# Eight more expert ups ahead of the dense stage, kept in row buffers

## The chip, the cores and the metric

The kernel runs on one core of a Trainium2 chip. The metric is the device time of one execution in microseconds, as the median of several runs. Engines are named as the profile names them: PE (TensorE matmuls), PEld (its weight loads), DVE (VectorE), ACT (ScalarE), POOL (GpSimd), SP (the queue that issues most transfers).

## What is computed

One decoder layer on 512 tokens of width 1024 in float32: a token sublayer (retention and forgetting attention, merged), and a channel sublayer, in which each token picks 128 of 16384 single-neuron experts by product keys. Cut to the second:

```
q  = (xc @ w_q).reshape(n, 8, 2, 128)
sc = einsum('nhcd,hckd->nhck', q, sub_keys)
s, idx = top_k(sc, 16)                       # per head and half
cand, cid = all 16 x 16 sums and expert numbers
top_s, pos = top_k(cand, 16);  eid = cid[pos];  gate = softmax(top_s)
hid = einsum('nhkd,nd->nhk', expert_u[eid], xc)
y   = einsum('nhk,nhkd->nd', gelu(hid) * gate, expert_v[eid])
h  <- LN(alpha*h + y + sigmoid(h W_g + b_g) * (p W_ple))
```

## The kernel before

The 512 tokens are four blocks of 128. The experts of the first two blocks are **gathered**: for each token and each of its 128 choices, POOL issues an indirect DMA that fetches one row of `peer_u` (128 tokens x 1024, 0.5 MB) into a row buffer, DVE multiplies it with x and sums it (L1087), later the same with `peer_v`, added to h (L1097). That makes 512 rows of each 0.5 MB. There are `ROWS` = 6 buffers "row", and, once the dense stage has begun, `MORE` = 2 further ones "more" (4 KB per partition each).

The last two blocks (256 tokens) run through **all** experts as dense products, in 128 blocks `b` of 128 experts each:

- `up(b)`: PE multiplies the block's `peer_u` with the 256 tokens (tile `hid`, 8 matmul instructions, which the trace shows as 16 records); ACT applies Gelu and writes the tile `a`. Two blocks share one 1 MB load `ur`, of which there are two buffers.
- `gate(b)`: DVE multiplies `a` with the dense gates `gw` of this block, and ACT rounds the product to `ah`.
- `load(b)` and `remainder`: ACT rounds the block's `peer_v` (1 MB load `vr` for two blocks) to `vh`, DVE writes the rest `vl`; likewise `al` from `a` and `ah`.
- `down(b)`: PE adds `ah*vh + ah*vl + al*vh` to four PSUM accumulators `acc` (12 matmuls).

The dense gates come from the routing: `select` (DVE, with a few ACT steps) makes the tiles `rt` for 128 tokens; PE transposes them (`gt`), ACT copies them to `tabs`, DVE builds one-hot masks `oa` and `ob` (`spread`), PE multiplies these (`gp`), ACT copies the products to `stg` and sends them to memory (`gd`), from where `gw` is loaded. This happens for one token block after the other.

`lead` ups are done before the dense loop, wherever `k.fill` puts them: between the query products, between the steps of `spread`, and the last four after it. `RES` = 4 more follow, straight into the accumulators' banks. The others run inside the loop over `b`. So the loop holds 128 - 44 - 4 = 80 ups.

On PE, DVE and POOL the order of instructions is that in which the code issues them. A small model in the kernel (`Clock`) keeps an estimate of the time of PE, DVE and the DMAs while the code is issued; `k.fill` issues an up when DVE is estimated over 2 us behind PE (`k.fill.when`), and `k.clock.row` issues a gathered row when DVE and the DMAs are estimated to have room. The order on ACT and SP is set by the compiler's scheduler.

Of the kernel before, what the change touches and what calls it, by code (L numbers as in the profile page):

```python
# [9 lines left out]
F32 = mybir.dt.float32  # L10
# [7 lines left out]
S, D, P = 512, 1024, 128  # L18
# [3 lines left out]
HEADS, K, NK = 8, 16, 128  # L22
# [109 lines left out]
class Clock:  # L132
# [3 lines left out]
    base, more = 0.07, 0.06  # L136
# [144 lines left out]
def norm_steps(k, dst, src, g, b, st=None, share=True):  # L281

    nc = k.nc
    mv = k.tp.tile([P, 2], F32, tag="ln_mv", name=k.uniq("mv"))
    rs = k.tp.tile([P, 1], F32, tag="ln_rs", name=k.uniq("rs"))
    if st is None:
        st = ln_tile(k)
        for i in range(2):
            ln_stats(k, st, i, src[:, i * 512:(i + 1) * 512])
        yield  # L290
    nc.vector.bn_aggr(mv, st)
    rstd(k, rs, mv[:, 1:2], 1)
    yield
    for i in (1, 0):
        sl = slice(i * 512, (i + 1) * 512)
        x = src[i] if isinstance(src, list) else src[:, sl]
        nc.vector.scalar_tensor_tensor(dst[:, sl], x, mv[:, 0:1], g[:, sl], op0=ALU.subtract, op1=ALU.mult)
        if i and share:
            nc.scalar.activation(dst[:, sl], dst[:, sl], AF.Copy, scale=rs)
            nc.gpsimd.tensor_tensor(dst[:, sl], dst[:, sl], b[:, sl], op=ALU.add)  # L300
        else:
            nc.vector.scalar_tensor_tensor(dst[:, sl], dst[:, sl], rs, b[:, sl], op0=ALU.mult, op1=ALU.add)
        yield
# [633 lines left out]
def by_slot(k, tr, routed):  # L937

    nc = k.nc
    ps = k.px.tile([P, 3, P], F32, tag="px", name=k.uniq("gt"))  # L940
    for i, src in enumerate(routed):
        nc.tensor.transpose(ps[:, i, :], src, k.ident)
    nc.scalar.activation(tr, ps, AF.Copy)
# [39 lines left out]
ROWS, MORE = 6, 2  # L983
XTRA = 2
RES = 4


class Experts:
# [7 lines left out]
    def up(self, b, ps=None):  # L996
        k, nc, ND = self.k, self.k.nc, self.ND
        if b % 2 == 0:
            self.uraw = k.us.tile([P, 2, 8, P], F32, tag="uraw", name=k.uniq("ur"))
            nc.sync.dma_start(self.uraw, k.I["uT"][b // 2])  # L1000
        if ps is None:
            ps = self.ph.tile([P, ND], F32, tag="hid", name=k.uniq("hid"))
        for c in range(8):
            nc.tensor.matmul(ps, self.uraw[:, b % 2, c, :], k.h1[:, c, :], start=c == 0, stop=c == 7)
        a = self.ap.tile([P, ND], F32, tag="a", bufs=self.lead + RES + XTRA, name=k.uniq("a"))
        nc.scalar.activation(a, ps, AF.Gelu)
        self.act[b] = a

# [91 lines left out]
def channel(k, dense, lead, ctx):  # L1100
    nc, tc, I = k.nc, k.tc, k.I
    gd = k.dr.tile([P, NK // GI, len(dense) * P // SG, GI * SG], F32, name="gd")
    ap = ctx.enter_context(tc.tile_pool(name="ap", bufs=2))
    k.us = ctx.enter_context(tc.tile_pool(name="us", bufs=2))
    ph = ctx.enter_context(tc.tile_pool(name="ph", bufs=2, space=PSUM))
    ex = Experts(k, dense, gd, lead, ap, ph)
    k.fill.items, k.fill.rate = [(ex.up, b) for b in range(lead)], 8
    k.fill.when = lambda: len(k.fill.items) > RES and k.clock.dve > k.clock.pe + 2
    k.clock.pace, k.clock.due, k.clock.base, k.clock.more = 4.2, k.clock.pe, 0.085, 0.115
    c0 = ExitStack()  # L1110
    with ExitStack() as c1:
        k.pp = c1.enter_context(tc.tile_pool(name="pp2", bufs=4, space=PSUM))
        k.px = c1.enter_context(tc.tile_pool(name="px2", bufs=2, space=PSUM))
        rp = c0.enter_context(tc.tile_pool(name="rp", bufs=2, side="right"))
        routed = [[rp.tile([P, HEADS * K], F32, bufs=1, name=f"rt{n}_{i}") for i in range(3)] for n in range(2)]
        with ExitStack() as c2:
            kp = c2.enter_context(tc.tile_pool(name="kp", bufs=2))
            s16, i16 = product_keys(k, REST, rp, kp, k.h1)
            k.side.items, k.side.rate = [select(k, rp, s16[:, 0], i16[:, 0], *routed[0])], 2.25
            embedding_gate(k, REST, k.h1, kp)  # L1120
            k.side.drain()
        with ExitStack() as c2:
            sps = [c2.enter_context(tc.tile_pool(name=f"sp{i}", bufs=1)) for i in range(2)]
            k.obs = k.slot([P, 2, 8, P], F32, "S2", "ob")
            tabs = k.fp.tile([P, 8, P], F32, tag="xg", bufs=FIRST.nt, name="tabs")
            k.iota = tabs[:, 6, :]
            nc.sync.dma_start(k.iota, I["iota"])
            k.side.items, k.side.rate = [select(k, rp, s16[:, 1], i16[:, 1], *routed[1])], 0.65
            for n in range(len(dense)):
                k.fill()  # L1130
                tr = tabs[:, 3 * n:3 * n + 3, :]
                by_slot(k, tr, routed[n])
                if n == len(dense) - 1:
                    c0.close()
                    dv = ctx.enter_context(tc.tile_pool(name="dv", bufs=2, side="right"))
                    for b in (0, 2):
                        ex.fetch(b, dv)
                for i, _ in enumerate(spread(k, sps, tr, n * P, gd, 4 if n else 8)):
                    k.clock.hold = n == len(dense) - 1 and i >= 28
                    k.tick()  # L1140
                k.side.drain()
            while k.fill.items:
                k.fill.step()
                k.clock.before()
    k.clock.before = lambda: None
    dl = ctx.enter_context(tc.tile_pool(name="dl", bufs=1))
    dp = ctx.enter_context(tc.tile_pool(name="dp", bufs=2))
    po = ctx.enter_context(tc.tile_pool(name="po", bufs=1, space=PSUM))
    acc = [[po.tile([P, 512], F32, name=f"acc{m}_{g}") for g in range(2)] for m in range(len(dense))]
    k.tp = dp  # L1150
    k.rows = [(k.gp, "row", ROWS)] * ROWS + [(k.gp, "more", MORE)] * MORE
    k.nrow = 0
    gb = k.slot([P, 2, D], F32, "S2", "gb2")
    g2, b2 = gb[:, 0, :], gb[:, 1, :]

    def finish(t):
        yield from norm_steps(k, k.h0[:, t, :], k.h0[:, t, :], g2, b2, share=False)
        nc.sync.dma_start(I["out"][t * P:(t + 1) * P, :], k.h0[:, t, :])
    for t in FIRST.blocks:
        at = max(0, len(k.feed.items) - (2 * P + 1) * (FIRST.end - 1 - t))  # L1160
        k.feed.items.insert(min(at + 24, len(k.feed.items)), finish(t))
    pace = len(k.feed.items) / (NK - 3)
    for b in range(2):
        ex.load(b, dl, dv)
    for i in range(RES):
        ex.up(lead + i, acc[i // 2][i % 2][:, :ex.ND])
    for b in range(2):
        ex.remainder(*ex.vw[b])
    k.feed(2)
    for b in range(3):  # L1170
        ex.gate(b, dl, dp)
    nc.sync.dma_start(g2, bcast(I["ln2_g"], D))
    nc.sync.dma_start(b2, bcast(I["ln2_b"], D))
    for b in range(2):
        ex.remainder(*ex.act[b])
    done = lead + RES
    for b in range(NK):
        if b + 2 < NK:
            ex.load(b + 2, dl, dv)
        while done < NK and done < lead + RES + (NK - lead - RES) * (b + 1) / (NK - 6):  # L1180
            ex.up(done)
            done += 1
        if b + 3 < NK:
            ex.gate(b + 3, dl, dp)
        k.feed(pace / 2)
        if b + 2 < NK:
            ex.remainder(*ex.vw[b + 2])
        k.feed(pace / 2)
        if b + 2 < NK:
            ex.remainder(*ex.act[b + 2])  # L1190
        if b < NK - 2:
            ex.down(b, acc, range(len(dense)))
        if b == 0:
            for m, t in enumerate(dense):
                for g in range(2):
                    nc.vector.tensor_tensor(acc[m][g], acc[m][g], k.h0[:, t, g * 512:(g + 1) * 512], op=ALU.add)
    assert not k.feed.items
    for m, t in enumerate(dense):
        for b in (NK - 2, NK - 1):
            ex.down(b, acc, (m,))  # L1200
        st = ln_tile(k)
        for g in range(2):
            ln_stats(k, st, g, acc[m][g])
        layer_norm(k, k.h0[:, t, :], acc[m], g2, b2, st=st, share=m < len(dense) - 1)
        for g in range(2):
            sl = slice(g * 512, (g + 1) * 512)
            nc.sync.dma_start(I["out"][t * P:(t + 1) * P, sl], k.h0[:, t, sl])
# [82 lines left out]
```

## Time and profile before

| | us |
|---|---|
| median of 3 runs | 1804.19 (1802.31 to 1805.01) |
| profiled execution, its own time | 1807.46 |
| its span | 1805.3 |
| PE busy | 1661.7 (92%) |
| DVE busy | 1378.1 (76%) |
| ACT busy | 600.1 (33%) |
| POOL busy | 633.2 (35%) |
| moved by DMA | 566.45 MB, 314 GB/s over the span |

Times in the trace are counted from the start of the span. The profile puts an engine's idle time down to what ended it, so "PE acc <- DVE al" is PE waiting for the tile `al` from DVE. Buffer numbers are left out there: `row` stands for every row buffer. The granted clock of PE was 0.972 on average. From 781 us on PE runs ups; the first gates' transposes start at 931 us, the second ones at 1045 us, the last `gp` ends at 1099.5 us, and the loop over the blocks begins at about 1135 us.

### The profile page before, as it was taken

To read this page: it belongs to the slowest core of one execution; us is meant where nothing else is said; L and a number is where in the kernel's file an instruction comes from. 1 tells how busy PE (TensorE), PEld (TensorE's weight loads), DVE (VectorE), ACT (ScalarE), POOL (GpSimd) and SP (SyncE) were. 2 spreads that over 40 slices of the span, in tenths; PEclk is the share of its full clock that TensorE was granted. 3 is DMA by queue.
4 is the path that set the end of the run, shared out by engine and by line. 5 is a ranking of instruction groups with operands and counts; after the bars stand their busy time and mean duration, and the time that the engine had idled before them with its cause. 6 is when DMAs were issued, how large, how long until landed. Compare 5 with 4: busy or idle time off the path is not lost.

```text
span 1805.3 us, 22411 instructions
## 1 busy us (share of the span) xinstructions
PE 1661.7 (92%) x7872; PEld 1330.5 (74%) x7872; DVE 1378.1 (76%) x2688; ACT 600.1 (33%) x1098; POOL 633.2 (35%) x524
## 2 busy tenths in 40 slices
PE   6999999998799999799949977999999999999995
PEld 4888996454656886488738966888888788788783
DVE  5654464697778888678988984787788788888888
ACT  4556643221023430111026674332323322332322
POOL 1000000025657555243443301334445444445441
PEclk9999999999899999999979999999999999999998
DMA  8544455879999999788876977999999999999993
GB/s 273 170 138 133 149 162 186 252 259 358 346 328 395 374 349 400 273 331 344 313 274 227 334 255 281 377 390 401 355 414 395 396 409 395 406 396 410 383 378 139
DMA packets 152992, 566.45 MB, mean 314 GB/s; under 512 B 18096, under 2 KB 34992, under 8 KB 134448
## 3 DMA queue, kind: packets, MB, share of 16 engines
q1 hardware_dynamic: 62496, 278.73, 42.0%
q0 software_dynamic: 73872, 269.52, 38.9%
q10 hardware_dynamic: 16512, 16.78, 2.7%
q8 instruction: 62, 1.02, 0.2%
q14 instruction: 50, 0.41, 0.1%
HBM read 543.99 MB, written 20.97 MB: 313 GB/s over the span
## 4 chain that ended last, share of the span: by engine, by line
PE 51%; issue 24%; DVE 10%; DMA 8%; ACT 3%; POOL 3%; SPq 1%; ACTq 0%; DVEq 0%; POOLq 0%
PE hid L194 20%; PE acc L194 17%; PE pj L194 8%; DVE h L1097 4%; DMA row<-in_peer_v,geu 3%; POOL row L1081 2%; PE gp L194 2%; PE lg L194 2%; DMA wr<-in_w_peer_q 2%; DVE s L194 1%; DMA row<-in_peer_u,geu 1%; DVE row L1087 1%; DVE i L194 1%; ACT vh L194 1%; DMA pw<-w 1%
## 5 line engine op out<-in xcount | busy, mean ns | idle before, releaser
L1081 POOL DMA_INDIRECT row<-in_peer_v,geu x256 | 320.5, 1252 | 389.0 <-DVE h L1097 324.7
L194 PE MATMUL hid<-h1f,ur 128*128 128x256 f32 x1984 | 449.9, 381 | 0.0
L1081 POOL DMA_INDIRECT row<-in_peer_u,geu x256 | 301.9, 1179 | 382.6 <-DVE row L1087 244.4
L194 PEld LDWEIGHTS hid<-h1f,ur 128*128 128x128 f32 x1984 | 378.4, 192 | 56.3 <-issue 3.8
L1097 DVE SCALAR_TENSOR_TENSOR h<-row,ghid,h 128x1024 f32<-128x1024 f32 x256 | 327.6, 1280 | 27.2 <-DMA row<-in_peer_v,geu 24.4
L1087 DVE SCALAR_TENSOR_TENSOR row<-row,xg 128x1024 f32<-128x1024 f32 x256 | 308.0, 1217 | 26.0 <-DMA row<-in_peer_u,geu 23.5
L194 DVE TENSOR_TENSOR vl<-vr,vh 128x1024 fp32r<-128x1024 f32 x128 | 156.8, 1226 | 107.5 <-ACT vh L194 107.5
L194 PE MATMUL acc<-vh,al 128*128 128x512 f32 x512 | 203.3, 397 | 21.7 <-DVE al L194 21.6
L194 PE MATMUL acc<-vh,ah 128*128 128x512 f32 x512 | 215.7, 421 | 0.0
L194 PE MATMUL acc<-vl,ah 128*128 128x512 f32 x512 | 201.7, 394 | 1.4 <-DVE vl L194 1.4
L194 DVE TENSOR_TENSOR wl<-wr,wh 128x1024 fp32r<-128x1024 f32 x72 | 88.1, 1223 | 85.9 <-ACT wh L194 85.7
L194 ACT ACTIVATE a<-hid 128x256 f32<-128x256 f32 x124 | 47.4, 382 | 299.9 <-PE hid L194 283.7
L194 ACT ACTIVATE vh<-vr 128x1024 fp32r<-128x1024 f32 x128 | 129.8, 1050 | 20.7 <-PE acc L194 18.9
L194 ACT ACTIVATE ah<-a 128x256 fp32r<-128x256 f32 x128 | 53.1, 416 | 242.3 <-DVE a L194 212.9
L194 PEld LDWEIGHTS acc<-vh,al 128*128 128x128 f32 x512 | 96.6, 189 | 48.9 <-DVE al L194 29.3
L194 PE MATMUL pj<-wr,h1f 128*128 128x512 f32 x256 | 120.7, 613 | 6.6 <-DMA wr<-in_w_peer_q 3.0
L194 PE MATMUL pj<-hT,wr 128*128 128x256 f32 x512 | 117.0, 385 | 0.1
L194 PEld LDWEIGHTS acc<-vl,ah 128*128 128x128 f32 x512 | 97.0, 189 | 24.2 <-DVE vl L194 3.3
L194 PEld LDWEIGHTS acc<-vh,ah 128*128 128x128 f32 x512 | 97.1, 190 | 18.8
L300 POOL TENSOR_TENSOR h<-h,b 128x512 f32<-128x512 f32 x6 | 8.2, 1388 | 291.7 <-ACT h L194 274.4
L194 PEld LDWEIGHTS pj<-hT,wr 128*128 128x128 f32 x512 | 97.3, 193 | 14.0 <-issue 1.4
L194 ACT ACTIVATE wh<-wr 128x1024 fp32r<-128x1024 f32 x72 | 76.2, 1058 | 93.5 <-PE pj L194 76.8
(231 smaller groups left out, 2489.3 us busy)
## 6 DMA issues: line engine op xcount, KB each, us to landing
ur<-in_uT SPq DMA_DIRECT2D x64, 1024.0 KB
vr<-in_vP SPq DMA_DIRECT2D x64, 1024.0 KB
wr<-in_w_in SPq DMA_DIRECT2D x104, 512.0 KB
wr<-in_w_peer_q SPq DMA_DIRECT2D x48, 512.0 KB
gd<-stg ACTq DMA_DIRECT2D x8, 2048.0 KB
gw<-gd SPq DMA_DIRECT2D x15, 1024.0 KB
wr<-in_w_ret_o SPq DMA_DIRECT2D x16, 512.0 KB
wr<-in_w_out SPq DMA_DIRECT2D x16, 512.0 KB
```

The lines of the kernel that those rows point to most:

```text
L194: return f(*a, **kw)
L300: nc.gpsimd.tensor_tensor(dst[:, sl], dst[:, sl], b[:, sl], op=ALU.add)
L1081: k.tc.nc.gpsimd.indirect_dma_start(out=r, out_offset=None, in_=src, in_offset=bass.IndirectOffsetOnAxis(ap=self.e[:, c:c + 1], axis=0))
L1087: self.k.tc.nc.vector.scalar_tensor_tensor(r, r, 1.0, self.x, op0=ALU.mult, op1=ALU.mult, accum_out=self.hid[:, c:c + 1])
L1097: self.k.tc.nc.vector.scalar_tensor_tensor(h1, r, self.hid[:, c:c + 1], h1, op0=ALU.mult, op1=ALU.add)
```

## The change

`lead` becomes 52. The ups of blocks 0 to 7 are the last eight of the lead instead of the first, and their results go into two tiles of four blocks each (`slab`), which take the two buffers "more" until these blocks are past; the pool of `a` keeps its 50 buffers. Until block 8 the gather therefore has six row buffers, and from there on all eight. The loop's 72 ups start at block 6, since the buffers of `a` come free only from block 8's end on, but for two. After the selection of the first gates the clock model's DVE time is put 20 us later, which makes `k.fill` issue ups there.

```
+SLAB = 8
...
-        a = self.ap.tile([P, ND], F32, tag="a", bufs=self.lead + RES + XTRA, name=k.uniq("a"))
+        if b < SLAB:
+            if b % 4 == 0:
+                self.slab = k.gp.tile([P, 4, ND], F32, tag="more", bufs=MORE, name=k.uniq("slab"))
+            a = self.slab[:, b % 4, :]
+        else:
+            a = self.ap.tile([P, ND], F32, tag="a", bufs=self.lead - SLAB + RES + XTRA, name=k.uniq("a"))
...
-    k.fill.items, k.fill.rate = [(ex.up, b) for b in range(lead)], 8
+    k.fill.items, k.fill.rate = [(ex.up, b) for b in (*range(SLAB, lead), *range(SLAB))], 8
...
             k.side.drain()
+            k.clock.dve += 20
...
-    k.rows = [(k.gp, "row", ROWS)] * ROWS + [(k.gp, "more", MORE)] * MORE
...
     for b in range(NK):
+        if b == SLAB:
+            k.rows = [(k.gp, "more", MORE)] * MORE + [(k.gp, "row", ROWS)] * ROWS
+            k.nrow = 0
...
-        while done < NK and done < lead + RES + (NK - lead - RES) * (b + 1) / (NK - 6):
+        while done < NK and done < lead + RES + (NK - lead - RES) * (b - SLAB + 3) / (NK - SLAB - 4):
...
-        decoder_layer(tc, aps, 44)
+        decoder_layer(tc, aps, 44 + SLAB)
```

Where it moves instructions. PE at the first gates' transposes, before (`hid` is an up, x8 its eight matmul instructions):

```order
L194 MATMUL hid_6508<-h1f,ur_6465 128x256 x8
L194 MATMUL hid_6546<-h1f,ur_6544 128x256 x8
L194 MATMUL gt_6557<-ident,rt_0_5440 128x128
L194 MATMUL gt_6557<-ident,rt_1_5441 128x128
L194 MATMUL gt_6557<-ident,rt_2_5442 128x128
L194 MATMUL gp_6572<-oa_6562,ob 128x128 x4
L194 MATMUL hid_6582<-h1f,ur_6544 128x256 x8
```

and after:

```order
L194 MATMUL hid_6546<-h1f,ur_6544 128x256 x8
L194 MATMUL hid_6557<-h1f,ur_6544 128x256 x8
L194 MATMUL hid_6570<-h1f,ur_6568 128x256 x8
L194 MATMUL hid_6581<-h1f,ur_6568 128x256 x8
L194 MATMUL hid_6594<-h1f,ur_6592 128x256 x8
L194 MATMUL hid_6605<-h1f,ur_6592 128x256 x8
L194 MATMUL hid_6618<-h1f,ur_6616 128x256 x8
L194 MATMUL gt_6629<-ident,rt_0_5440 128x128
L194 MATMUL gt_6629<-ident,rt_1_5441 128x128
L194 MATMUL gt_6629<-ident,rt_2_5442 128x128
L194 MATMUL gp_6653<-oa_6634,ob 128x128 x4
L194 MATMUL hid_6663<-h1f,ur_6616 128x256 x8
```

Six ups have come between the last up of before and the transposes. DVE at the same place, from the end of `rt` to the first masks, before:

```order
L194 TENSOR_TENSOR rt_2_5442<-rt_2_5442,gsm_6530 128x128
L1097 SCALAR_TENSOR_TENSOR h_68<-row_6563,ghid_2841,h_68 128x1024
L194 TENSOR_TENSOR oa_6562<-tabs 128x1024
L194 TENSOR_TENSOR ob<-tabs 128x1024
L194 TENSOR_TENSOR oa_6568<-tabs 128x1024
```

and after (L1103 is the former L1097, a gathered row):

```order
L194 TENSOR_TENSOR rt_2_5442<-rt_2_5442,gsm_6530 128x128
L1103 SCALAR_TENSOR_TENSOR h_68<-row_6635,ghid_2841,h_68 128x1024
L1103 SCALAR_TENSOR_TENSOR h_68<-row_6638,ghid_2841,h_68 128x1024
L1103 SCALAR_TENSOR_TENSOR h_68<-row_6641,ghid_2841,h_68 128x1024
L1103 SCALAR_TENSOR_TENSOR h_68<-row_6644,ghid_2841,h_68 128x1024
L194 TENSOR_TENSOR oa_6634<-tabs 128x1024
L194 TENSOR_TENSOR ob<-tabs 128x1024
```

Three more rows stand ahead of the masks; over both spreadings six more rows are issued before the dense loop. ACT there, before (`sg` is the embedding gate's Sigmoid, the last `rt` row an Exp, `a` a Gelu):

```order
L194 ACTIVATE a_6555<-hid_6546 128x256
L194 ACTIVATE w_6460<-iff_6154 128x1024
L194 ACT_TABLE_LOAD
L194 ACTIVATE sg_6343<-sg_6343 128x512 x2
L194 ACT_TABLE_LOAD
L194 ACTIVATE rt_2_5442<-rt_2_5442 128x128
```

and after:

```order
L194 ACTIVATE a_6566<-hid_6557 128x256
L194 ACTIVATE w_6460<-iff_6154 128x1024
L194 ACTIVATE a_6579<-hid_6570 128x256
L194 ACTIVATE a_6590<-hid_6581 128x256
L194 ACTIVATE a_6603<-hid_6594 128x256
L194 ACTIVATE a_6614<-hid_6605 128x256
L194 ACT_TABLE_LOAD
L194 ACTIVATE sg_6343<-sg_6343 128x512 x2
L194 ACT_TABLE_LOAD
L194 ACTIVATE a_6627<-hid_6618 128x256
L194 ACT_TABLE_LOAD
L194 ACTIVATE rt_2_5442<-rt_2_5442 128x128
```

The last of the new Gelus stands between the Sigmoid and the Exp, with one table load more. Further on PE has 19 ups, not 18, between the first group's `gp` and the second transposes, and two, not one, in the second group's spreading. In the loop its order was, with H an up and d a block's products, `H d H d d H d H d d H d H d d ...`, and is now `d d d d d d H d H d d H d H d d H d d H ...`.

## The prediction

> **What bounds the kernel now.** I read the stretches first, cut at the places the change touches, with the busy time of each engine, the granted clock, the DMA share and the rate. Columns: PE, PEld, DVE, ACT and POOL busy with instruction counts.
>
> ```profile
> 921.50:951.50 30.00, 1.45 (x4) 0.55 (x3) 25.34 (x36) 7.22 (x13) 14.67 (x11) 0.57 0.69 254
> 951.50:1045.50 94.00, 93.71 (x547) 85.76 (x547) 85.47 (x152) 65.31 (x178) 33.80 (x23) 0.97 0.83 298
> 1045.50:1099.50 54.00, 38.45 (x274) 35.13 (x275) 49.94 (x102) 39.82 (x103) 0.00 (x0) 0.94 0.65 221
> 1099.50:1135.30 35.80, 30.42 (x131) 25.85 (x130) 9.56 (x18) 6.05 (x15) 10.72 (x11) 0.90 0.91 347
> 1135.30:1186.90 51.60, 51.60 (x234) 43.96 (x233) 41.30 (x69) 15.90 (x27) 19.75 (x18) 1.00 0.96 382
> 1186.90:1758.50 571.60, 557.24 (x2490) 468.96 (x2489) 470.20 (x668) 178.89 (x297) 267.00 (x222) 1.00 0.99 394
> ...
> 1117.50:1777.00 659.50, 636.67 (x2829) 534.28 (x2827) 535.45 (x769) 202.97 (x338) 303.84 (x254) 0.99 0.98 390
> 1300.00:1310.00 10.00, 9.44 (x43) 7.64 (x41) 6.86 (x13) 3.39 (x6) 3.75 (x4) 1.00 1.03 417
> ```
>
> Row 1 is the wait for the first gates: PE does 1.45 us in 30 while DVE works 25.3. In row 2, the first group's spreading, PE is full. In row 3, the second group's, DVE is (49.9 of 54). Row 4 is the tail of ups. Rows 5 and 6 are the blocks: PE is busy 608.8 of 623.2 us. There one up less is one up's time less, as long as DVE and the DMAs, at 0.99, keep up. The last two rows are the transfers of tail and blocks together, and the highest rate that I found in 10 us. From the chain in order of time, an up and a block's products:
>
> ```profile
> 1135.46 3.45 PE hid L194 x16
> ...
> 1154.03 2.73 PE acc L194 x12
> ```
>
> An up is 3.45 us, a block 2.73. After the change the loop holds 72 ups, not 80.
>
> **Part 1, the wait before the first gates.** Timeline rows of PE, then DVE, then ACT around it:
>
> ```profile
> 914.51 7.07 PE L194 MATMUL hid<-h1f,ur 128*128 128x256 f32 x32
> 931.09 0.45 PE L194 MATMUL gt<-ident,rt 128*128 128x128 f32 x1 [9.52 <-DVE rt L194]
> 946.52 0.47 PE L194 MATMUL gt<-ident,rt 128*128 128x128 f32 x1 [14.98 <-DVE rt L194]
> 951.55 2.04 PE L194 MATMUL gp<-oa,ob 128*128 128x128 f32 x8 [3.06 <-DVE ob L194]
> ```
>
> ```profile
> 933.26 6.55 DVE L1097 SCALAR_TENSOR_TENSOR h<-row,ghid,h 128x1024 f32<-128x1024 f32 x5
> ...
> 947.81 1.28 DVE L1097 SCALAR_TENSOR_TENSOR h<-row,ghid,h 128x1024 f32<-128x1024 f32 x1
> 949.04 1.23 DVE L194 TENSOR_TENSOR oa<-tabs 128x1024 f32<-128x1024 f32 x1
> ```
>
> ```profile
> 930.98 1.06 ACT L194 ACTIVATE w<-iff 128x1024 f32<-128x1024 f32 x1 [8.98 <-DVE rt L194]
> 932.05 1.28 ACT L194 ACT_TABLE_LOAD   x1
> 942.87 1.22 ACT L194 ACTIVATE sg<-sg 128x512 f32<-128x512 f32 x2 [9.53 <-DVE sg L194]
> 944.11 1.28 ACT L194 ACT_TABLE_LOAD   x1
> 946.70 0.31 ACT L194 ACTIVATE rt<-rt 128x128 f32<-128x128 f32 x1 [1.30 <-DVE rt L194]
> ```
>
> Before, one of the seven ups already stands ahead of the transposes; six are new there: 6 x 3.45 = 20.7 us from 921.5. There are two PSUM buffers, so the fourth new up needs the second's, and the second's Gelu now stands behind w on ACT, until 932.05: evacuated at 932.4, it costs PE 0.7. The sixth ends at 942.9, and PE then waits for the same DVE instruction as before (946.5). ACT gets one table load more, since the last of these Gelus comes between the Sigmoid and the Exp: 944.1 + 1.28 + 0.38 + 1.28 = 947.1 instead of 946.70, 0.4 later. DVE now takes four rows, not one, between rt and the first mask oa: 3 x 1.3 = 3.9. So the first gp comes at 951.55 + 0.4 + 3.9, **4.3 later**. Three more ur loads (3.1 MB) fall into these 30 us. They moved 254 GB/s where others reach 417, so there is room for 4.9 MB: I take nothing, with 3 us as the upper end (one 1 MB load ahead of DVE's rows, 2.5 us at 417 GB/s); below zero it can hardly go, as DVE's order stays.
>
> The Trainium skill's page "ScalarE: Activation LUTs", What ACT_TABLE_LOAD costs, gives about 1.28 us and 1.38 more for a drain, 2.66 per switch; by that the Exp would be 3.2 us late instead of 0.4, and the sum 2.8 worse. Here the load that ACT starts at 957.50 is followed by the next instruction at 958.80:
>
> ```profile
> 957.50 1.28 ACT L194 ACT_TABLE_LOAD   x1
> 958.80 0.38 ACT L194 ACTIVATE a<-hid 128x256 f32<-128x256 f32 x1
> ```
>
> so I keep 1.28.
>
> **Part 2, the two spreadings.** The first gets 19 ups, not 18: **+3.45**, as PE is full there. DVE gets two further rows beside the three above, 2.6 us, against 8.5 us that it idles: covered. The second gets one row more, in a stretch that DVE bounds, 1.3, and two ups, not one, ahead of its early units:
>
> ```profile
> 1056.89 4.63 PE L194 MATMUL gp<-oa,ob 128*128 128x128 f32 x40
> 1057.98 1.23 DVE L194 TENSOR_TENSOR ob<-tabs 128x1024 f32<-128x1024 f32 x1 [3.05 <-PE gp L194]
> 1061.94 1.22 DVE L194 TENSOR_TENSOR ob<-tabs 128x1024 f32<-128x1024 f32 x1
> ```
>
> The second up stands between the next unit's two gp groups (0.9 each): they end at 1057.8 + 0.9 + 3.45 + 0.9 = 1063.1, and the ob at 1061.94 waits for it, 1.2. Together **+2.5** (1.3 to 4.8, a whole up).
>
> **Part 3, the first blocks.** The tail (4 ups, 4 more into acc, the trip of gd to gw) keeps its order. But blocks 0 to 5 now have no up between them. DVE's cycle for one block, start to start:
>
> ```profile
> 1151.40 0.42 DVE L194 TENSOR_TENSOR al<-a,ah 128x256 fp32r<-128x256 f32 x1
> 1151.74 0.47 DVE L194 TENSOR_TENSOR a<-a,gw 128x256 f32<-128x256 f32 x1
> 1152.14 1.21 DVE L1087 SCALAR_TENSOR_TENSOR row<-row,xg 128x1024 f32<-128x1024 f32 x1
> 1153.28 1.21 DVE L194 TENSOR_TENSOR vl<-vr,vh 128x1024 fp32r<-128x1024 f32 x1
> 1154.42 1.21 DVE L1087 SCALAR_TENSOR_TENSOR row<-row,xg 128x1024 f32<-128x1024 f32 x1
> 1155.56 0.42 DVE L194 TENSOR_TENSOR al<-a,ah 128x256 fp32r<-128x256 f32 x1
> ```
>
> 4.16 us against PE's 2.73. Block 0 starts 3.45 us earlier than before, without its up, at 1135.3 of the old clock; al of blocks 3, 4 and 5 then comes about 1143.2, 1147.3 and 1151.5, and PE waits 0.9 for block 4 and 1.5 for block 5. From block 6 on ups stand between and PE is the later one again: **+2.4** (0 to 6 x 1.43 = 8.6).
>
> The row buffers are six until block 8, not eight. With six, in the stage ahead (780 to 1100), the waits are
>
> ```profile
> DVE h L1097 <- DMA row<-in_peer_v,geu: 11.6, 9, 2.7
> ```
>
> 11.6 us in 320; for some 36 us, 1.3. I take **+1.3**, between 0 and 8 x 2.7 - 5 = 16.6, if each of eight blocks meets the longest of these waits (the 5 are DVE's lead: at 4.16 a block al of block 9 is there at 1168, and PE, with three ups by then, reaches it at 1173); the low end is nearer, since the rows' share of the DMA is the same there.
>
> **Part 4, the loop.** 8 ups of 80 leave: **-27.6**. PE's waits in row 6 are all of one kind:
>
> ```profile
> PE acc L194 <- DVE al L194: 14.3, 15, 1.0
> ```
>
> 0.97 us, at pairs of blocks with no up between, where ACT has both vh copies behind an up's Gelu. Such places in ACT's order go from 27 to 28, pairs with pairs on both sides from 4 to 16. I take **+1.5**, from 0 to 13 more of them, 12.4: the count of 28 is the nearest row to what pays now.
>
> DMA: 659.5 us at 390 GB/s are 257 MB. Four ur loads (4.2 MB) and six rows (3.1 MB) leave; 250 MB in 634 us need 394. The peak of 417 covers that, and no wait of PE or DVE for a transfer stands in row 6: 0 in the sum.
>
> **Sum**: 4.3 + 3.45 + 2.5 + 2.4 + 1.3 - 27.6 + 1.5 = **-12.1**. The profiled execution took 1807.46 us (span 1805.3), 3.3 above the median of the three runs, 1804.19; the difference carries over: **1792**.
>
> **Rivals.** *The transfers bound the blocks.* For it: 0.98 of the DMA time is taken. Against it: 417 in single stretches, and no engine waits for one. If the mean cannot pass 390, 250 MB take 641 us, 18.7 saved of 25: 6.5 worse, 1798.5.
> "DMA: Bandwidth & Descriptors", Bandwidth, of the Trainium skill puts HBM at about 358 GB/s for a core of a pair and 425 measured for one alone; by 358 the blocks would be transfer-bound already and the gain less than half. The row at 417 speaks for the second.
>
> *The remainders give it back; the slower side.* PE's order has 43 pairs of blocks between two ups (41 before). If each paid 0.97 instead of 15 of them, that is 28 waits more, 27.2 us instead of my 1.5: +13.6, 1818. It decides at 29 waits (no gain) and makes a slower kernel from 33. For it: DVE's 4.16 per block is near PE's 4.45 for two blocks and an up. Against it: DVE idles 101 us in row 6, and only places with ACT's copies late pay now.
>
> *The change does not do what it says*: PE cannot run the six ups in the wait, as their Gelus stand behind ACT's wait for sg. Only the last does, and PE waits for rt then anyway; were all six to run after 947, the first gp would come 20.7 us later still, and the sum be +8.6, 1813.
>
> **Numbers.** The forecast's case 0.58, alone 1785 to 1797; transfers 0.17; better than the sum (no waits in parts 3 and 4, about 1787 or less) 0.06; partly given back, within 0.2% (3.6 us, about what a measurement tells apart) 0.12; slower 0.07. Faster 0.81, same 0.12, slower 0.07. The range leaves out the two end cases and what lies between them and the middle: 1783 to 1801.
>
> **What would show it.** Between the last pj and the first gp, PE busy some 22 us instead of 1.45, and the first gp about 4 us later; the last gp about 10 later; from there to the end some 22 less than before; PE's waits for al near 16 in the loop. Wrong if those waits exceed 26 us, if DVE waits for rows in blocks 0 to 7, or if PE waits for ur among the six.

## The result, and the profile after

The changed kernel takes 1796.04 us (median of 6 runs, 1790.88 to 1799.45), the kernel before beside it 1806.03 us (6 runs, 1802.31 to 1810.02). The ratio is 0.9939, with a 95% interval of 0.9925 to 0.9952: 11 us less, between 8.7 and 13.6. The forecast was 1792, from a sum of -12.1 on a median of 1804.19; 1.8 of the 4 us between are the kernel before, which stands that much higher over six runs. The profiled execution took 1793.62 us (span 1791.9). The stretches, cut at the same events as before (same columns: PE, PEld, DVE, ACT and POOL busy with counts, granted clock, DMA share, GB/s):

```profile
921.50:957.80 36.30, 22.26 (x96) 18.44 (x94) 27.63 (x37) 10.41 (x19) 17.00 (x13) 0.87 0.78 304
957.80:1055.40 97.60, 97.03 (x562) 88.41 (x563) 87.85 (x156) 66.38 (x179) 36.49 (x26) 0.98 0.84 306
1055.40:1110.25 54.85, 42.69 (x289) 39.38 (x290) 51.05 (x107) 39.65 (x104) 0.94 (x1) 0.91 0.69 243
1110.25:1145.90 35.65, 30.41 (x134) 25.89 (x133) 9.55 (x18) 6.41 (x16) 8.86 (x9) 0.95 0.92 349
1145.90:1187.50 41.60, 40.13 (x178) 33.08 (x177) 39.18 (x65) 13.90 (x21) 24.88 (x19) 1.00 0.98 388
1187.50:1745.00 557.50, 541.39 (x2415) 453.91 (x2415) 464.81 (x660) 178.06 (x293) 255.96 (x217) 1.00 1.00 397
```

Row 1: PE is busy 22.26 us where it was 1.45, so the six ups do run in the wait. But the wait is 36.3 us long, not 30. Row 2 is 3.6 longer, with PE full. Row 3, where DVE is the bound, hardly changed. Rows 5 and 6 are the blocks, with 72 ups instead of 80. By stages, from the two profiles (in us from the start of the span, then lengths):

| | before | after | difference | forecast |
|---|---|---|---|---|
| first `gp` | 951.6 | 957.8 | +6.2 | +4.3 |
| first `gp` to second transposes | 93.9 | 97.6 | +3.7 | +3.45 |
| second transposes to last `gp` | 53.9 | 54.7 | +0.8 | +2.5 |
| last `gp` to the end | 705.9 | 681.8 | -24.1 | -22.4 |

The first gates come later than foreseen. In the timeline of after, PE, then ACT, then DVE there:

```profile
914.77 9.23 PE L194 MATMUL hid<-h1f,ur 128*128 128x256 f32 x42
925.36 14.05 PE L194 MATMUL hid<-h1f,ur 128*128 128x256 f32 x64 [1.36 <-DMA ur<-in_uT]
942.11 5.19 PE L194 MATMUL hid<-h1f,ur 128*128 128x256 f32 x16 [2.70 <-DMA ur<-in_uT]
947.13 0.38 PE L194 MATMUL gt<-ident,rt 128*128 128x128 f32 x2
950.36 0.30 PE L194 MATMUL gt<-ident,rt 128*128 128x128 f32 x1 [2.85 <-DVE rt L194]
957.79 2.04 PE L194 MATMUL gp<-oa,ob 128*128 128x128 f32 x8 [7.13 <-DVE ob L194]
```

```profile
947.33 0.38 ACT L194 ACTIVATE a<-hid 128x256 f32<-128x256 f32 x1 [3.73 <-PE hid L194]
947.73 1.28 ACT L194 ACT_TABLE_LOAD   x1
949.02 0.31 ACT L194 ACTIVATE rt<-rt 128x128 f32<-128x128 f32 x1
```

```profile
944.65 0.29 DVE L194 TENSOR_TENSOR rt<-tops 128x128 f32<-128x128 f32 x1
949.37 0.28 DVE L194 TENSOR_REDUCE gsm<-rt 128x8 f32<-128x128 f32 x1 [4.43 <-ACT rt L194]
...
950.13 5.24 DVE L1103 SCALAR_TENSOR_TENSOR h<-row,ghid,h 128x1024 f32<-128x1024 f32 x4
955.29 1.22 DVE L194 TENSOR_TENSOR oa<-tabs 128x1024 f32<-128x1024 f32 x1
```

PE waits 1.36 and 2.70 us for `ur`. The sixth up so ends at 947.3, its Gelu stands ahead of the Exp on ACT, and DVE, which had `rt` ready at 944.9, waits 4.43 us for that Exp. Then it takes the four rows, 5.24 us, before the first mask. In row 6, the blocks, this line of the waits of PE (us in total, times, longest) stands against before's 14.3, 15, 1.0:

```profile
PE acc L194 <- DVE al L194: 16.0, 16, 1.0
```

### The profile page after: what moved, and what is told of

The parts are those of the page before. It is cut to its first block, busy times and chain, and to the rows that moved or that the text cites. A ratio compares the mean times of both kernels' runs of the same rounds, so it can differ in the third digit from the quotient of the medians.

```text
span 1791.9 us, 22410 instructions
## 1 busy us (share of the span) xinstructions
PE 1664.2 (93%) x7872; PEld 1328.5 (74%) x7872; DVE 1377.8 (77%) x2688; ACT 601.9 (34%) x1099; POOL 633.5 (35%) x524
## 4 chain that ended last, share of the span: by engine, by line
PE 60%; issue 18%; DVE 10%; DMA 7%; ACT 3%; POOL 1%; SPq 1%; ACTq 0%; DVEq 0%; POOLq 0%
PE hid L194 20%; PE pj L194 18%; PE acc L194 16%; DVE h L1103 3%; DMA wr<-in_w_peer_q 2%; PE lg L194 2%; DMA ur<-in_uT 1%; DVE row L1093 1%; PE gp L194 1%; DVE ob L194 1%; DVE oa L194 1%; DMA gd<-stg 1%; ACT vh L194 1%; PE ry L194 1%; SPq L194 1%
## 5 line engine op out<-in xcount | busy, mean ns | idle before, releaser
L1103 DVE SCALAR_TENSOR_TENSOR h<-row,ghid,h 128x1024 f32<-128x1024 f32 x256 | 327.5, 1279 | 25.4 <-DMA row<-in_peer_v,geu 19.2
L194 ACT ACTIVATE vh<-vr 128x1024 fp32r<-128x1024 f32 x128 | 129.9, 1051 | 18.2 <-PE acc L194 12.2
```

The lines of the kernel that those rows point to most:

```text
L194: return f(*a, **kw)
L1103: self.k.tc.nc.vector.scalar_tensor_tensor(h1, r, self.hid[:, c:c + 1], h1, op0=ALU.mult, op1=ALU.add)
```

## The experiments

Each ran in five rounds beside the kernel before, which stood at medians of 1805.56, 1806.74 and 1806.22 us in the three groups of four. Ratios are to that. Times of stages are from one profiled execution of each kernel, and executions of one kernel spread by up to 10 us, so a difference of a few us between two profiles is not yet one between two kernels. Some are counted from the end of the last `pj`, PE's last products for the embedding gate: the last event ahead of the gates that all the kernels share. "Ups" counts those ahead of the first transposes, in the first spreading, in the second, in the tail, and in the loop: before 21, 18, 1, 4, 80; after 27, 19, 2, 4, 72 (each time 4 more go into the accumulators).

**What filling the wait is worth, and what an up costs elsewhere.** First the change without the six ups in the wait (21, 18, 9, 4, 72):

```
-            k.clock.dve += 20
```

> The changed kernel without the 20 us that the clock model's DVE time is put later: the eight ups of slabs and the six row buffers stay, but no new up stands ahead of the first gates' transposes; 18 ups stay in the first spreading and 9, not 2, fall into the second. Theory A (an up gains where PE waits, and the place decides): the 30 us wait comes back with PE at about 1.5 us busy; the second spreading, where PE has 15.5 us idle, takes 8 ups of 27.6 us and some 9 rows more, and grows by 12 to 18 us; the rest gains 24 as in the changed kernel. Sum -6 to -12 against the kernel before, some 1796 to 1800, so 0 to 6 worse than the changed one. Rival B (the gain is the filled wait alone): no gain, 1804 or more. Rival C (only the count of ups in the loop matters): the same as the changed kernel within 2 us.

Measured: 1795.57 us, 0.9946 [0.9932, 0.9959], the same as the change with them: 10 less than before, within theory A's 6 to 12, but in total also what rival C said. The stages tell the two apart: the places do cost, and the costs balance. The ups went into the second spreading instead, which took 69.9 us, not 54.7. The first `gp` came at 949.0, 8.8 earlier. So what the change gains does not come from the 30 us wait: with it, the later gates and one more up in the first spreading cost nearly as much (8.8 and 3.5) as the second spreading saves (15.2).

The opposite, the kernel before with only the six ups in the wait (27, 13, 0, 4, 80):

```
+            k.clock.dve += 20
```

> The kernel before with only the 20 us put on the clock model's DVE time: 27 ups, not 21, ahead of the first transposes, 13 instead of 18 in the first spreading, none instead of one in the second, 80 in the loop as before. Theory A: PE works in the wait, the first gp comes about 6 us later as in the changed kernel, the first spreading loses five ups (17 us of PE) but falls only to what DVE needs, 85 to 90 of its 94 us, and the loop is unchanged: between -4 and +3 us, no difference that counts. Rival B (the filled wait is the gain): -10 or better.

Measured: 1811.78 us, 1.0039 [1.0025, 1.0052]: slower by 6, where the theory went to +3 at most and the rival expected a gain. The two spreadings:

```profile
957.20:1049.80 92.60, 80.23 (x467) 73.31 (x467) 79.41 (x146) 64.17 (x175) 20.87 (x15) 0.95 0.68 240
1049.80:1096.00 46.20, 35.69 (x257) 33.25 (x258) 45.18 (x97) 37.06 (x97) 0.00 (x0) 0.93 0.67 228
```

With five ups fewer (17 us of PE's time), and six gathered rows fewer, the first is only 1.3 shorter than before: with 13 ups PE has 12 us idle in it and DVE 13. So PE's fullness there, on which I had costed it, was an effect of the ups put in to fill it. That the order of masks and rows sets the stage is the likely reading; it was not tried by itself. The last `gp` came 3.4 earlier than before, but six rows more were left for the loop: from block 0 to the start of the last up it took 623.0 us, not 616.2. How much of this is the rows was not separated.

**What an up of the loop is worth.** The kernel before with eight of the loop's ups left out, in four pairs; their activations are a Gelu of other data, so ACT's work stays:

```
+SKIP = (56, 57, 72, 73, 88, 89, 104, 105)
...
+        if b in SKIP:
+            a = self.ap.tile([P, ND], F32, tag="a", bufs=self.lead + RES + XTRA, name=k.uniq("a"))
+            nc.scalar.activation(a, k.h1[:, 0, :], AF.Gelu)
+            self.act[b] = a
+            return
```

> The kernel before with eight of the loop's 80 ups left out (blocks 56, 57, 72, 73, 88, 89, 104 and 105: no load of their experts and no products; their Gelu reads another tile, so the output is not the layer's). It prices an up in the loop by itself, with eight row buffers and ups from block 0 on. Theory A (PE bounds the loop): 8 x 3.45 = 27.6 us less, minus up to 4 for waits on al where four or more blocks follow each other: -23 to -28, 1776 to 1781. Rival (the transfers bound it): -10 to -13, four loads of 1 MB at 390 GB/s. Rival (DVE's remainders give it back): less than -14.

Measured: 1793.69 us, 0.9934 [0.9920, 0.9947]: 12 us for eight ups of 3.45, as both rivals said. The timeline of PE where a pair is missing:

```profile
1435.30 0.50 PE L194 MATMUL acc<-vh,al 128*128 128x512 f32 x1 [0.95 <-DVE al L194]
...
1438.41 0.50 PE L194 MATMUL acc<-vl,ah 128*128 128x512 f32 x1 [0.30 <-DVE vl L194]
...
1439.89 0.50 PE L194 MATMUL acc<-vh,al 128*128 128x512 f32 x1 [0.98 <-DVE al L194]
...
1444.04 0.50 PE L194 MATMUL acc<-vh,al 128*128 128x512 f32 x1 [0.99 <-DVE al L194]
```

Blocks without an up follow one another here at DVE's pace (1439.89 to 1444.04, 4.15 us, where PE needs 2.73), and PE waits in each. That left three explanations: an up is worth only half, the transfers bound the loop (four 1 MB loads at 390 GB/s are 10.8 us), or it was the clumping. So, as many ups left out, but one in ten, and the other 72 spread evenly:

```
-SKIP = (56, 57, 72, 73, 88, 89, 104, 105)
+SKIP = (52, 62, 72, 82, 92, 102, 112, 122)
...
-        while done < NK and done < lead + RES + (NK - lead - RES) * (b + 1) / (NK - 6):
+        while done < NK and made < lead + RES + (NK - lead - RES - len(SKIP)) * (b + 1) / (NK - 6):
             ex.up(done)
+            made += done not in SKIP
             done += 1
```

> The kernel before with eight ups of the loop left out (their activations are then a Gelu of other data on ACT, so the output is not the reference's), one in ten, and the other 72 spread evenly over the blocks: the loop has as many ups as the changed kernel's, with no work put elsewhere. The run that left them out in pairs gained 12 us. Theory (an up of the loop is worth its 3.45 us where the ups left are spread, and the pairs left runs of four or five blocks in which DVE's 4.16 per block is the bound): 20 to 27 us faster than before. Rival (the loop is bound near its present length by something else, DVE's rows or the transfers, so that an up is worth half): 10 to 14 us faster.

Measured: 1785.09 us, 0.9876 [0.9854, 0.9898], 22 us: the theory's range, if not the full 27.6. But this run changes more than the spread. The blocks left out are all even, and the even block issues the load for two, so eight loads fall away here and four with the pairs (the odd blocks use what the buffer still holds). The loads of the pairs' run, then of this one (count, KB each, median us to landing):

```profile
ur<-in_uT SPq DMA_DIRECT2D x60, 1024.0 KB, 8.4
ur<-in_uT SPq DMA_DIRECT2D x56, 1024.0 KB, 8.1
```

At 390 GB/s eight loads are 21.5 us and four 10.8, close to the 22 and 12 measured. The traces speak against that reading. From block 0 to the start of the last up PE is busy 577.8 us of 597.1 in this run and 579.1 of 603.4 with the pairs, and the rest of both is waits for DVE; from 1145 to 1740 us neither PE nor DVE nor ACT waits for a transfer in either run. Even ups with only four loads fewer were not run. PE's waits from block 0 to the last up, for the pairs, then for one in ten:

```profile
PE acc L194 <- DVE al L194: 22.8, 24, 1.0
PE acc L194 <- DVE vl L194: 1.5, 5, 0.3
```

```profile
PE acc L194 <- DVE al L194: 18.9, 19, 2.1
PE acc L194 <- DVE vl L194: 0.3, 1, 0.3
```

These waits are 5.1 us of the 6.3 by which the two profiles differ in that stretch; from the last `gp` to the end they differ by 8.1.

**The row buffers.** The kernel before with six row buffers throughout:

```
-    k.rows = [(k.gp, "row", ROWS)] * ROWS + [(k.gp, "more", MORE)] * MORE
```

> The kernel before with six row buffers throughout instead of eight, nothing else changed. It prices the two buffers that the change takes away until block 8. Theory (the buffers are cheap where DVE isn't short of rows): over the whole loop DVE waits for rows a few times more and PE is covered: 0 to +4 us. Rival (rows as late as the longest waits for them seen, 2.7 us, some ten times): +10 to +25, and the changed kernel pays a part of it.

Measured: 1804.50 us, 0.9987 [0.9972, 1.0002]. Two buffers less cost nothing, even over the whole loop, though DVE then waits for rows there (1187.5 to 1745 us), which it does not in the kernel before:

```profile
DVE h L1097 <- DMA row<-in_peer_v,geu: 13.6, 13, 1.8
DVE row L1087 <- DMA row<-in_peer_u,geu: 9.2, 7, 3.0
```

PE's time from block 0 to the last up stays at 616 us. The end of 16.6 us that I had kept for the buffers falls.

**What delays the first gates.** The change with no row ahead of the first group's masks:

```
                 tr = tabs[:, 3 * n:3 * n + 3, :]
+                k.clock.hold = n == 0
                 by_slot(k, tr, routed[n])
```

> The changed kernel with the gathered rows held back from the first transposes until the first step of spreading is through: no row, instead of four, stands on DVE between the first gates and the first masks; seven ups stay ahead. Theory A (those rows are on the path to the first gp): the first gp comes 5 us earlier, and since DVE has as much work up to the second gates, part of it is given back there: -2 to -5 us against the changed kernel. Rival (DVE's total up to the second gates sets the time, not the order): within 1 us of the changed kernel, with the second transposes where they were.

Measured: 1784.15 us, 0.9884 [0.9868, 0.9901]: 21 us faster than before, twice the change, and the fastest kernel of the study. Against the change that is 12, where I had expected 2 to 5. PE, ACT, DVE there:

```profile
941.44 3.69 PE L194 MATMUL hid<-h1f,ur 128*128 128x256 f32 x16 [0.74 <-DMA ur<-in_uT]
...
951.56 2.05 PE L194 MATMUL gp<-oa,ob 128*128 128x128 f32 x8 [3.07 <-DVE ob L194]
```

```profile
945.17 0.38 ACT L194 ACTIVATE a<-hid 128x256 f32<-128x256 f32 x1 [0.28 <-PE hid L194]
945.57 1.28 ACT L194 ACT_TABLE_LOAD   x1
946.86 0.31 ACT L194 ACTIVATE rt<-rt 128x128 f32<-128x128 f32 x1
```

```profile
947.20 0.28 DVE L194 TENSOR_REDUCE gsm<-rt 128x8 f32<-128x128 f32 x1 [0.98 <-ACT rt L194]
...
949.06 1.23 DVE L194 TENSOR_TENSOR oa<-tabs 128x1024 f32<-128x1024 f32 x1 [1.01 <-ACT tabs L194]
```

The first `gp` is 6.2 earlier than after's. Two things did that: the four rows are gone from the path (5.2, of which 1.0 returns as a wait for `tabs`), and the last `ur` came earlier (PE's wait 0.74, not 2.70), so that DVE waits 0.98 us for the Exp, not 4.43. From the last `gp` on, the loop brought another 4.0, with 15 waits for `al` instead of 18.

Next I took the load's size. The change with one 0.5 MB `ur` load per block into four buffers:

```
-        if b % 2 == 0:
-            self.uraw = k.us.tile([P, 2, 8, P], F32, tag="uraw", name=k.uniq("ur"))
-            nc.sync.dma_start(self.uraw, k.I["uT"][b // 2])
+        uraw = k.us.tile([P, 8, P], F32, tag="uraw", name=k.uniq("ur"))
+        nc.sync.dma_start(uraw, k.I["uT"][b // 2, :, b % 2])
...
-    k.us = ctx.enter_context(tc.tile_pool(name="us", bufs=2))
+    k.us = ctx.enter_context(tc.tile_pool(name="us", bufs=4))
```

> The changed kernel with the ups' weights loaded block by block (0.5 MB into one of four buffers) instead of two blocks at a time (1 MB into one of two): the same bytes. Theory (PE waited 4.1 us for ur among the six ups, the last up's Gelu so came late, the Exp behind it, and DVE waited 4.4 for that): a half load is there earlier, PE's waits for ur ahead of the first gates go to under 1 us, the first gp comes 2 to 4 us earlier than the changed kernel's and the whole is 2 to 6 us faster than it. Rival (the rate of the transfers limits it, whatever their size): PE waits as long for ur, within 2 us of the changed kernel.

Measured: 1796.54 us, 0.9935 [0.9916, 0.9955]: no different from the change. The theory was right in one step and no more. PE no longer waits for `ur`; it waits for ACT:

```profile
PE hid L194 <- ACT a L194: 3.9, 1, 3.9
```

```profile
936.02 1.06 ACT L194 ACTIVATE w<-iff 128x1024 f32<-128x1024 f32 x1 [9.03 <-DVE rt L194]
936.98 0.64 ACT L194 ACTIVATE a<-hid 128x256 f32<-128x256 f32 x2
...
950.48 0.38 ACT L194 ACTIVATE a<-hid 128x256 f32<-128x256 f32 x1
950.88 1.28 ACT L194 ACT_TABLE_LOAD   x1
952.17 0.31 ACT L194 ACTIVATE rt<-rt 128x128 f32<-128x128 f32 x1
```

With `ur` there early, PE fills both `hid` buffers and stands until `w`, ahead of the Gelus on ACT, is through. This is the wait that the prediction had priced at 0.7. It takes the place of the transfer's, and the last Gelu is as late as before, counted from the last `pj` (34.3 us, 33.7 in the change). But that is no longer what holds the gates: DVE waits 0.78 us for the Exp, not 4.43. DVE is late itself. Its `rt` is ready 35.5 us after the last `pj`, not 31.3, as it takes nine rows, not seven, between that `pj` and `w` and waits longer for them. Why more rows stand there with the load split was not tried. Both edits together:

> The changed kernel with both: no row ahead of the first group's masks, and the ups' weights loaded block by block. Theory (the two delays of the first gates add up: three rows ahead of the first masks, and ur loads that come late): 3 to 5 us faster than with the rows held alone, which took 1784.15: 1779 to 1781. Rival (with the rows held, the Exp's lateness is taken by other work, or the split costs in the loop): within 2 us of 1784.

Measured: 1789.57 us, 0.9900 [0.9880, 0.9919]. Neither expectation is met: slower than the rows held alone by its median, and the intervals overlap. The split adds nothing; here too DVE's `rt` comes late (35.9 us after the last `pj`, 31.4 with the rows held alone), and the first `gp` 4.2 later.

The other way to have the Exp in time is one up less ahead of it, which goes into the second spreading (26, 19, 3, 4, 72):

```
-            k.clock.dve += 20
+            k.clock.dve += 16
```

> The changed kernel with five new ups, not six, ahead of the first gates' transposes; the sixth moves into the second spreading. Theory (the sixth's Gelu comes between Sigmoid and Exp, with a table load on each side, and DVE waited 4.4 us for that Exp): DVE's wait for the Exp falls under 1.5, the first gp is 3 us earlier counted from the last pj, and the up costs up to 3.45 in the second spreading: within 3 us of the changed kernel's 1796. Rival (the Exp's lateness is on the path to the end and the up in the second spreading is free): 4 to 6 us faster than it.

Measured: 1793.93 us, 0.9934 [0.9920, 0.9948], the same as the change, as the theory had it. DVE's wait for the Exp fell to 0.4 us, and the first `gp`, counted from the end of the last `pj`, came 40.6 us after it instead of 44.2. The second spreading took 58.2 us, not 54.7. An up moved out of the wait costs 3.5 there, its whole length.

**Whether the pieces add up.** Rows held, without the six ups in the wait (the two edits above, on the change):

> The changed kernel without the six ups ahead of the first gates (the eight ups are kept in the two buffers all the same, and stand in the second spreading and behind), and with no row ahead of the first group's masks. With the rows held, filling the wait is the only difference to the run that took 1784.15. Theory (filling the wait pays once no row is moved ahead of the masks with it: the six ups then don't stand in the second spreading, where they cost most of what they cost anywhere): 1790 to 1796, 6 to 12 slower than that run and within 3 of the run that only took the fill away, 1795.57. Rival (the wait's fill is worth nothing, and all that was gained there came from the rows): 1782 to 1787.

Measured: 1798.75 us, 0.9959 [0.9945, 0.9972]; above the theory's range, and far from the rival's. Against 1784.15 this is what the fill with six ups is worth once no row is moved ahead with it: the ratios differ by 0.0075, some 13 us. By the profiles the last `gp` is 12.2 later (1103.9 and 1116.1); 1.9 of this lies ahead of the last `pj`, where the code is the same.

The rows held on the kernel before:

> The kernel before with no row ahead of the first group's masks (one stood there) and nothing else. It prices that edit without the change. Theory (one row of 1.3 leaves the path to the first gates; later rows are as many): 0 to -3 us against before. Rival (the order of the rows in the spreading or the loop that comes with it is what gained 11 us on the changed kernel): -8 to -12.

Measured: 1804.87 us, 0.9990 [0.9980, 1.0000], 1.4 less by the medians: one row of 1.3 on the path, as expected. The edit has nothing to give without the ups.

Five ups in the wait and the rows held:

> Five new ups and no row ahead of the first group's masks. Theory (with the rows held and the ur loads in time the sixth up delays the Exp by 1 us only, so that taking it out gains nothing and the up costs elsewhere): 1784 to 1788. Rival (the Exp still sets the first gates): 1780 to 1783.

Measured: 1797.45 us, 0.9948 [0.9933, 0.9963]: a miss of 9 us or more for both expectations. From the last `pj` to the first `gp` it takes 36.8 us, as with six ups and rows held (36.8), and 3.8 less than with five ups alone. Against the fastest kernel it loses 4.3 in the second spreading (the up that stands there), 6.1 in the loop, and 2.5 ahead of the last `pj`, where the code is the same.

The six kernels with and without the fill, and with and without rows ahead of the masks, stand like this, from the end of the last `pj` to the last `gp` in the profile, then the median:

| ups in the wait | rows as issued | no row ahead of the masks |
|---|---|---|
| none | 199.5, 1795.57 | 199.1, 1798.75 |
| five | 196.2, 1793.93 | 192.8, 1797.45 |
| six | 196.5, 1796.04 | 188.8, 1784.15 |

Up to the last gates the fill is worth 3 us with rows on the path and 6 to 10 without, and the rows held are worth more the more ups stand there. The medians show it for six ups alone: with none and with five, the kernel with the rows held measured 3 us slower (the intervals of the ratios overlap). With none there is little to gain; with five, the profiles lose 2.9 us again behind the last `gp`, and 3.1 lie ahead of the last `pj`, where the code is the same.

**The waits of the loop.** The runs with 72 ups have the same loop, but PE's waits for `al` come out at 15 to 20. From block 0 to the start of the last up, by each profile; "excess" is the length less 616.2, plus 3.45 for each up that the loop has less between these two events:

| | waits for `al` | length | excess |
|---|---|---|---|
| before | 15 | 616.2 | 0 |
| before, rows held | 14 | 615.1 | -1.1 |
| before, six row buffers | 14 + 1 | 616.1 | -0.1 |
| before, six ups in the wait | 15 + 2 | 623.0 | 6.8 |
| rows held | 15 | 592.4 | 0.4 |
| rows held, `ur` split | 17 | 593.9 | 1.9 |
| no ups in the wait | 17 | 594.7 | 2.7 |
| no ups in the wait, rows held | 17 | 594.7 | 2.7 |
| `ur` split | 18 | 595.3 | 3.3 |
| the change | 18 | 596.4 | 4.4 |
| five ups | 19 | 597.4 | 5.4 |
| five ups, rows held | 20 | 598.5 | 6.5 |
| 8 ups left out, even | 19 + 1 | 597.1 | 8.5 |
| 8 ups left out, in pairs | 24 + 5 | 603.4 | 14.8 |

(The number behind the plus counts waits for `vl`, with the six ups in the wait one of them for `vh`; the last two rows have eight ups less there, the changed ones seven.) The excess takes an up at its 3.45; that price is put in, not found by the table. By it each further wait goes with some 0.9 to 1.7, where the idle time of one is 0.97. The run with six ups in the wait, which has six rows more in its loop, does not fit: 6.8 with two waits more. Part of the difference shows in the rows above: the matmul behind a wait takes 0.50 us, where others of its shape take 0.39.

## Why the prediction was right, and where it was not

*The first gates: the term that was mis-sized.* +4.3 was +6.2 by the profile, or +7.3 counted from the last `pj`. The three further rows and their 3.9 us were right. "I take nothing" for the `ur` loads was wrong: PE waited 4.1 us for them, beyond the 3 us that I had set as an upper end, since a load took 8 to 9 us. Two of them in the chain in order of time:

```profile
917.12 8.11 DMA ur<-in_uT
...
932.54 9.44 DMA ur<-in_uT
```

I had compared a rate over the whole wait with the highest rate, 417 GB/s, where a latency counts: two buffers, and an up that needs one of them whole. And "0.4 later" for the Exp assumed that the sixth up was done by 942.9. It ended at 947.3, and the Exp began at 949.02, 2.3 later than before. That the last Gelu stands ahead of the Exp was in the working; that a late `ur` passes through it to DVE was not. The prediction named "if PE waits for ur among the six" as a sign of error, and it was one.

ACT's table load itself came as taken: 947.73, and the next instruction 1.29 later. The rule of the Trainium skill ("ScalarE: Activation LUTs", What ACT_TABLE_LOAD costs), 2.66 us with its drain, is not borne out by this row either.

*The spreadings.* First +3.7 for +3.45, second +0.8 for +2.5. Here the sum counted one cost twice. The `ob` behind the second up starts 5.24 us after the one before it (1067.48 and 1072.72), where it was 3.96, but the further row of 1.2 us, priced beside the up, stands in that same gap (DVE takes two rows, from 1069.65 to 1071.9, where it took one), so DVE does not wait for `gp` there; its one wait for `gp` in this stage is 2.6 us, before 3.1:

```profile
1067.48 1.22 DVE L194 TENSOR_TENSOR ob<-tabs 128x1024 f32<-128x1024 f32 x1 [2.64 <-PE gp L194]
...
1069.65 1.21 DVE L1093 SCALAR_TENSOR_TENSOR row<-row,xg 128x1024 f32<-128x1024 f32 x1
...
1070.79 1.22 DVE L1093 SCALAR_TENSOR_TENSOR row<-row,xg 128x1024 f32<-128x1024 f32 x1
...
1072.72 1.23 DVE L194 TENSOR_TENSOR ob<-tabs 128x1024 f32<-128x1024 f32 x1
```

For the first spreading, the run with six ups in the wait alone shows that "PE is full there" was no reason to price ups at 3.45 in both directions: the five taken out saved 1.3. The term was right for an up added.

*The first blocks.* PE waits for `al` twice in blocks 0 to 5, 0.49 and 0.98 us: 1.5 instead of 2.4, from the same cycle of DVE (4.16 a block). For the six row buffers the sum had 1.3. From block 0 to 1190 us DVE waits this much for rows, and PE loses nothing by it:

```profile
DVE row L1093 <- DMA row<-in_peer_u,geu: 2.2, 2, 1.9
```

Both waits come at 1180.8 and 1184.6 us, with PE at blocks 8 and 9, so just behind the blocks that the prediction had named for its sign. The run with six row buffers throughout has none in this stretch. More likely it is the step from the slabs to rows in the same buffers: the row issued at 1169.81 had waited 2.1 us on POOL for a slab's `al`.

*The loop.* From block 0 to the last up it fell by 19.8 us. The forecast's terms from there are the eight ups less the 3.45 that lie ahead of block 0, that is -24.15, and +2.4, +1.3 and +1.5: -18.95. An up left out was worth 2.7 us one in ten and 1.5 in pairs, by the medians, not 3.45; here seven fewer gave 19.8 of 24.15. "A few more of 0.97" was three more from block 0 on, but with an excess of 4.4: by that account each costs more than its idle time.

*The rivals.* Transfers do not bound the blocks: 397 GB/s in row 6, above the 390 that this rival took for the cap and the 394 of before's row, and PE and DVE wait for none there. (In blocks 4 and 5 ACT waits for `vr` twice, 5.7 us, without a wait of DVE or PE behind it that names ACT.) The Trainium skill ("DMA: Bandwidth & Descriptors", Bandwidth) gives about 358 GB/s for a core beside which the other of its pair streams too, and 425 measured for one alone: the row lies above the first and below the second. The remainders' rival asked for 28 further waits; three came. The mechanism itself is seen all the same: clumped ups brought 14 more waits of both kinds, and of the 27.6 us of eight ups 12 were gained. How much of the rest is the clumping stays open, as the run with spread ups also has four loads less. "The change does not do what it says" fell with PE's 22.26 us in the wait.

By the two profiles the total is -13.4 for the sum's -12.1: +1.9 and +0.3 up to the second transposes, -1.7 in the second spreading and -1.7 behind it. The errors cancel in part; that the total came this near is to that extent luck.

*Open.* What of the 11 us between the change and the rows held belongs to the edit. Shown by the five-up pair are 3.8 from the last `pj` to the first `gp`, 1.0 of it given back in the first spreading. The rest is an Exp 3.45 us less late, since `ur` came earlier (whether because the rows' fetches leave it room or by chance was not tried), and 4.0 in the loop with three waits less. Nor is it shown why one order of the same loop has 15 of these waits and another 20, or how far the number varies from execution to execution: each is of one profile. Which of the few versions is fastest can so not be foreseen from the ups' places alone.

## What to carry to other kernels

Work put into an engine's wait is worth only what it leaves elsewhere, less what it pulls onto the path: here six ups filled 21 of 30 idle us and gained nothing in the whole until the gathered rows that moved with them were kept off the path, and then 13. That was not robust: with five ups and the rows held it was 1, though the gates came 6 us earlier. Before pricing such a fill, follow the last piece through the in-order queue of the next engine (its Gelu ahead of the Exp) and price its loads by their duration, not by the mean rate. Where two engines are close, as PE's 4.45 and DVE's 4.16 per block here, work taken out in clumps was worth less than half its length (12 of 27.6 us) and spread out 22, a part of which may be the loads that went with it.

## What the runs showed of the hardware

After a wait of 2.7 us PE ran at half its clock for a while: the granted clock was 0.50 from 941.75 to 945.10 us, and the 16 matmuls at 942.11 took 5.19 us, where they take 3.6. Behind a wait of 0.74 us, in the run with the rows held, it stayed at 1.00 and they took 3.69. Two 1 MB loads beside gathered rows took 8.1 and 9.4 us each, while the core moved 304 GB/s over that wait; the median of a kernel's `ur` loads of this size is 8.1 to 8.5 us in ten of the profiles. The last `pj`, ahead of which these kernels do the same work, ended between 911.2 and 920.5 us in twelve of the profiles, so one profile settles when a stage starts to some 5 us only; counting from the last common event takes most of that out. The rest is some 2 us: with the same code from there on, the first `gp` of five profiles comes 35.1 to 36.9 us after the last `pj`.
